# Output tiles of an fp32 batched product, stored head by head instead of with two heads alternating

## The chip, the cores and the metric

The kernel runs on one core of a Trainium2 chip. The metric is the device time of one execution in microseconds (us): before the change the median of three runs is 301.21 us (301.14 to 301.47). Engines are named as in the profile: PE (TensorE matmul), DVE (VectorE), ACT (ScalarE), POOL (GpSimd), SP (SyncE, which here only issues transfers). A "transfer" is one DMA instruction; the core has 16 DMA engines that carry its packets.

## The reference

```python
def setup_inputs():
    batch, n_heads, seq_t, seq_s, channels = 8, 12, 512, 512, 64
    ...
def reference(x, y):
    return np.einsum('bhtc,bhsc->bhts', x, y).astype(np.float32)
```

There are 8 x 12 = 96 heads. For each head, a 512 x 64 matrix x is multiplied by the transpose of a 512 x 64 matrix y, which gives 512 x 512 floats (1 MiB). Inputs are 25.17 MB together, the output is 100.66 MB. The arithmetic runs in bf16 with fp32 sums; inputs and output are fp32 in DRAM.

## The kernel before

**Tiling.** The 96 heads are cut in 6 groups of 16 (`NG`), and each group in two halves of 8 heads, 12 halves in all (`NH`). A load brings one group of x or of y as 128 partitions of 4096 floats: 8 partitions a head (`Q`), 64 rows of 64 channels in each. Each half then makes 4 output tiles (`V`), each for two heads that lie four heads (4 MiB of output) apart; the two are called u = 0 and u = 1. That makes 48 output tiles. An output tile has 128 partitions, and each holds 8 consecutive rows of one head (`K`), 4096 floats or 16 KiB that are contiguous in DRAM. 64 partitions belong to one head of the pair and 64 to the other.

**Staging of x.** ACT casts a loaded x tile to bf16 (`compress`, tile `xk`). `mix` copies it, in four parts of 32 partitions for each half, into `xb`, on POOL for the first two halves and on DVE for the others. `xb` was set to zero once, and each part writes only the places of its own u, so that the matrix has blocks of zeros: one matmul over 128 contraction rows then serves both heads of a pair without mixing them. `transposes` makes `xT` from `xb` on DVE in 32 x 32 blocks of 32-bit words. A word is two bf16 values, and the two stay side by side: before the change they are the places of u = 0 and u = 1, so the columns of `xT`, and with them the rows of an output tile, alternate between the two heads.

**Staging of y.** y tiles are cast to bf16 into `yb` by ACT, DVE and POOL, and DVE transposes them into `yT` in the same manner.

**Products and stores.** PE runs a loop (`all_products`) of 8 matmuls of 128 x 512 for an output tile, four into each of two PSUM buffers (`pm`). ACT copies each buffer into one half of a slot (`result`, 128 x 2048 floats), and SP then stores the whole slot in one transfer of 2 MiB (`store`). There are 5 slots (`SLOTS`); loads and stores share them in turn.

**Order.** The order is written out by hand: loads, casts and mixes of the 12 input tiles, with the first four results woven in, then the rest of the results, four for each half, with `prepare` (transposes of one half, mixes of the next) after every fourth. `emit` derives the semaphore waits from the tiles that an instruction reads and writes. All 60 transfers are issued by SP on one queue, the 12 loads ahead of the 48 stores. A slot is written again by ACT only when the store from it has landed.

**Lines that the change touches.** `ov` (the view of the output that a store writes), `mix` (L123 holds the copy itself), `transposes` (L188 for x, L197 for y), and `products`, which only names what a product reads. The store is issued at L233, the loads at L139; the eviction by ACT is L245, the matmul L223.

Of the kernel before, what the change touches and what calls it, by code (L numbers as in the profile page):

```python
# [9 lines left out]
def kernel(  # L10
# [22 lines left out]
    nc = tc.nc  # L33
    B, H, T, C = x.shape
    _, _, S, _ = y.shape
    P = 128
    G = 16
    Q = P // G
# [3 lines left out]
    V = G // 4  # L42
    K = 8
    E = R // K
    D = 32
# [3 lines left out]
    bf16 = mybir.dt.bfloat16  # L49
# [4 lines left out]
    xv = x.rearrange("b h t c -> (b h t c)").rearrange("(g p n) -> g p n", p=P, n=R * C)  # L54
    yv = y.rearrange("b h t c -> (b h t c)").rearrange("(g p n) -> g p n", p=P, n=R * C)
    ov = out.rearrange("b h t s -> (b h t s)").rearrange(
        "(o u h q n) -> o h q u n", u=2, h=V, q=Q * E, n=K * S
    )

    sb = ctx.enter_context(tc.tile_pool(name="sb", bufs=1))  # L60
# [2 lines left out]
    xks = [sb.tile([P, R, C], bf16, name=f"xk{i}") for i in range(NG - 1)]  # L63
    ybs = [[sb.tile([P, R // 2 * D], u32, name=f"yb{h}{i}") for i in range(NG - 1 + h)] for h in range(2)]
    xbs = [sb.tile([P, K * E * D], u32, name=f"xb{half}") for half in range(2)]
    xTs = [sb.tile([P, K * D * E], u32, name=f"xT{i}") for i in range(2)]
# [5 lines left out]
    def need(name, points, known_by=None):  # L72

        best = {}
        for p, v in points:
            if known[name].get(p, 0) < v:
                best[p] = max(best.get(p, 0), v)
        for p, v in list(best.items()):
            if any(snaps[q, w].get(p, 0) >= v for q, w in best.items() if q != p):
                del best[p]  # L80
        if known_by is not None:
            assert all(p in dict(known_by) and v <= dict(known_by)[p] for p, v in best.items())
        for p, v in best.items():
            if known_by is None:
                engines[name].wait_ge(sems[p], v)  # L85
            known[name][p] = v
            for q, w in snaps[p, v].items():
                known[name][q] = max(known[name].get(q, 0), w)
# [3 lines left out]
    def emit(name, make, reads=(), writes=(), dma=None, lane=None, known_by=None):  # L92

        points = [writer[r] for r in (*reads, *writes) if r in writer]
        points += [v for w in writes for v in readers.get(w, ())]
        if name == "pool" and name in ticks:
            points.append((name, ticks[name]))
        need(name, points, known_by)
        p, step = (lane or name, 1) if dma is None else (f"dma{dma}", 16)
        if p not in sems:  # L100
            sems[p] = tc.alloc_semaphore(p)
        if make is not None:
            make().then_inc(sems[p], step)
        at = (p, ticks.get(p, 0) + step)
        ticks[p] = at[1]
        snaps[at] = {**known[name], p: at[1]}
        if dma is None:
            for q in lanes.get(name, (name,)):
                snaps[at][q] = ticks.get(q, 0)
        for r in reads:  # L110
            readers.setdefault(r, []).append(at)
        for w in writes:
            writer[w], readers[w] = at, []
# [4 lines left out]
    def copy(name, dst, src, reads, writes):  # L118
        emit(
            name,  # L120
            lambda: nc.scalar.activation(dst, src, COPY)  # L121
            if name == "act"
            else engines[name].tensor_copy(dst, src),  # L123
            reads,
            writes,
        )
# [41 lines left out]
    def mix(i, name, part):  # L168

        g, half = divmod(i, 2)  # L170
        ch, u = divmod(part, 2)
        lo = half * 64 + u * D
        xk = g % (NG - 1)
        xv2 = xbs[half].bitcast(bf16).rearrange("p (k e c u) -> p k e c u", k=K, e=E, u=2)
        copy(
            name,
            xv2[part * D:(part + 1) * D, :, :, :, u],
            xks[xk][lo:lo + D, :, ch * D:(ch + 1) * D].rearrange("p (e k) c -> p k e c", k=K),
            [("xk", xk)],
            [("xb", half, part)],  # L180
        )

    def transposes(i):
        g, half = divmod(i, 2)
        b = g % (NG - 1 + half)
        emit(
            "dve",
            lambda: nc.vector.transpose(  # L188
                xTs[half].rearrange("p (k r e) -> p k e r", k=K, e=E),
                xbs[half].rearrange("p (k e c) -> p k e c", k=K, e=E),  # L190
            ),
            [("xb", half, part) for part in range(4)],
            [("xT", half)],
        )
        emit(
            "dve",
            lambda: nc.vector.transpose(  # L197
                yTs[half].rearrange("p (r j) -> p j r", r=D),
                ybs[half][b].rearrange("p (j c) -> p j c", c=D),
            ),  # L200
            [("yb", half, b, ch) for ch in range(2)],
            [("yT", half)],
            lane="tr",
        )

    def products(o, k):
        evicted = 2 * o + k // 4 + 1
        emit("pe", None, [("xT", o // V % 2), ("yT", o // V % 2)], [("pm", k // 4)],
             known_by=[("ev", evicted), ("tr", o // V + 1)])

    def all_products():
# [26 lines left out]
    def result(o, s):  # L238

        for k in range(0, K, 4):  # L240
            pm = k // 4
            products(o, k)
            emit(
                "act",
                lambda: nc.scalar.activation(  # L245
                    slots[s][:, k * S:(k + 4) * S], pms[pm].rearrange("p j s -> p (j s)"), COPY
                ),
                [("pm", pm)],
                [("slot", s, pm)],
                lane="ev",  # L250
            )
        store(o, s)

    def prepare(i):

        if i < NH:
            transposes(i)
        if i + 1 < NH:
            for part in range(4):
                mix(i + 1, "dve", part)  # L260

    with tc.tile_critical():  # L262
# [12 lines left out]
        for n in range(2 * NG):  # L275
            if n == 11:
                result(3, slot())
            compress(n)
            mix(n // 4, "pool", n % 4)
            if n == 4:  # L280
                transposes(0)
            if n < 5:
                load(n + SLOTS)
            elif n in (6, 8):
                load(n // 2 + 7)
            elif n < 10:
                front.append(slot())
            if n > 7 and n < 11:
                result(n - 8, front[n - 8])
            if n == 9:  # L290
                transposes(1)
# [38 lines left out]
```

## Time and profile before

| What | Value |
|---|---|
| Median of three runs | 301.21 us (301.14 to 301.47) |
| The profiled execution's own time | 301.22 us |
| Its span, first to last instruction | 299.2 us |
| ACT busy | 211.8 us (71%) |
| DVE busy | 151.9 us (51%) |
| PE busy | 139.6 us (47%) |
| POOL busy | 56.1 us (19%) |
| Moved by DMA | 125.85 MB, mean 421 GB/s |
| One store, issue to landing (median) | 20.8 us |

The profiled execution lies on the median, so its durations can be set against the median directly; 301.22 - 299.2 = 2.0 us lie outside the span. An engine's busy share is a mean over the span. "Issue to landing" of a store contains the time that it stands behind earlier transfers in the queue. A waiting engine is named with what released it.

### The profile page before, as it was taken

The numbers are of one execution on the slowest core, as the hardware profiler recorded it, in microseconds if no ns is written. First come the engines' busy times: TensorE is split into PE (matmuls) and PEld (weight loads), VectorE is DVE, ScalarE is ACT, GpSimd is POOL, SyncE is SP. The second block draws the span as 40 slices with busy tenths as digits, with TensorE's granted clock in tenths as the row PEclk, the third lists the DMA queues.
The fourth block names the chain that finished last, engine by engine and source line by source line (L and its number), as shares of the span: only waits on it lengthen the run. The fifth ranks groups of instructions, "written<-read, shape, count | busy, mean of one in ns | idle before, by whom it ended". The sixth has DMA issues, their size and how long they took to land.

```text
span 299.2 us, 1282 instructions
## 1 busy us (share of the span) xinstructions
PE 139.6 (47%) x384; PEld 36.1 (12%) x384; DVE 151.9 (51%) x73; ACT 211.8 (71%) x109; POOL 56.1 (19%) x23
## 2 busy tenths in 40 slices
PE   0000040547666655566676465666475766473000
PEld 0000010111111111111111111111111111110000
DVE  2167897999839594907609349086291510000000
ACT  1665676999999998686867677777767686868000
POOL 2399999991000000000000000000000000000000
PEclk9999995657789997867756857756957766957555
DMA  7999999999999999999999999999999999999995
GB/s 278 425 436 427 429 427 432 427 429 425 436 436 423 431 436 424 432 438 425 429 440 426 425 438 431 421 427 436 431 425 425 423 431 429 427 425 425 429 427 237
DMA packets 8642, 125.85 MB, mean 421 GB/s; under 512 B 960, under 2 KB 960, under 8 KB 960
## 3 DMA queue, kind: packets, MB, share of 16 engines
q1 hardware_dynamic: 8640, 125.83, 98.9%
q14 instruction: 2, 0.02, 0.0%
HBM read 25.17 MB, written 100.66 MB: 421 GB/s over the span
## 4 chain that ended last, share of the span: by engine, by line
DMA 61%; ACT 23%; issue 4%; PE 2%; DVE 2%; SPq 0%; ACTq 0%
DMA out_dram<-slot 48%; ACT slot L245 20%; DMA slot<-in_y_dram 7%; DMA slot<-in_x_dram 6%; PE pm L223 2%; DVE yb L123 2%; ACT xk L121 1%; ACT yb L121 1%; SPq L139 0%; ACTq L85 0%; SPq L325 0%; SPq L262 0%
## 5 line engine op out<-in xcount | busy, mean ns | idle before, releaser
L245 ACT ACTIVATE slot<-pm 128x2048 f32<-128x2048 f32 x96 | 174.2, 1885 | 43.2 <-DMA out_dram<-slot 42.5
L223 PE MATMUL pm<-yT,xT 128*128 128x512 bf16 x384 | 139.6, 509 | 134.9 <-ACT slot L245 97.8
L188 DVE STREAM_TRANSPOSE xT<-xb 128x2048 uint32<-128x2048 uint32 x12 | 46.7, 3896 | 69.4 <-PE pm L223 67.0
L223 PEld LDWEIGHTS pm<-yT,xT 128*128 128x128 bf16 x384 | 36.1, 115 | 237.5 <-ACT slot L245 161.1
L123 DVE COPY xb<-xk 32x2048 bf16<-32x2048 bf16 x36 | 46.9, 1303 | 1.0
L123 DVE CAST yb<-slot 64x2048 bf16<-64x2048 f32 x12 | 36.2, 3016 | 17.1 <-DMA slot<-in_y_dram 16.8
L123 POOL COPY xb<-xk 32x2048 bf16<-32x2048 bf16 x12 | 36.3, 3022 | 10.5 <-ACT xk L121 9.7
L121 ACT ACTIVATE xk<-slot 128x4096 bf16<-128x4096 f32 x6 | 21.7, 3617 | 16.3 <-DMA slot<-in_x_dram 16.3
L197 DVE STREAM_TRANSPOSE yT<-yb 128x1024 uint32<-128x1024 uint32 x12 | 23.1, 1928 | 0.0
L121 ACT ACTIVATE yb<-slot 64x2048 bf16<-64x2048 f32 x6 | 14.8, 2463 | 5.2 <-DMA slot<-in_y_dram 5.1
L123 POOL CAST yb<-slot 64x2048 bf16<-64x2048 f32 x6 | 17.8, 2973 | 1.3 <-DMA slot<-in_y_dram 0.8
L271 DVE MEMSET xb<- 128x2048 uint32 x1 | 1.8, 1765 | 1.4 <-SPq L262 1.4
L121 ACT ACT_TABLE_LOAD x1 | 1.3, 1283 | 1.0 <-SPq L262 1.0
L271 POOL MEMSET xb<- 128x2048 uint32 x1 | 1.8, 1805 | 0.5 <-SPq L262 0.5
L314 POOL MEMSET const-float32-0.0<- 128x1 f32 x1 | 0.1, 98 | 0.2 <-issue 0.2
L314 POOL MEMSET const-float32-1.0<- 128x1 f32 x1 | 0.1, 98 | 0.0
L314 POOL MEMSET const-bfloat16-1.0<- 128x1 bf16 x1 | 0.1, 98 | 0.0
L314 POOL MEMSET const-uint8-127<- 128x1 uint8 x1 | 0.1, 98 | 0.0
## 6 DMA issues: line engine op xcount, KB each, us to landing
out_dram<-slot SPq DMA_DIRECT2D x48, 2048.0 KB, 20.8
slot<-in_x_dram SPq DMA_DIRECT2D x6, 2048.0 KB, 17.7
slot<-in_y_dram SPq DMA_DIRECT2D x6, 2048.0 KB, 20.8
```

The costliest lines, as they stand in the source:

```text
L121: lambda: nc.scalar.activation(dst, src, COPY)
L123: else engines[name].tensor_copy(dst, src),
L188: lambda: nc.vector.transpose(xTs[half].rearrange("p (k r e) -> p k e r", k=K, e=E), xbs[half].rearrange("p (k e c) -> p k e c", k=K, e=E),),
L197: lambda: nc.vector.transpose(yTs[half].rearrange("p (r j) -> p j r", r=D), ybs[half][b].rearrange("p (j c) -> p j c", c=D),),
L223: last = nc.tensor.matmul(pms[pm][:, b, :], xT[:, 4 * pm + b, h, :], yT[:, h * S:(h + 1) * S], start=True, stop=True,)
L245: lambda: nc.scalar.activation(slots[s][:, k * S:(k + 4) * S], pms[pm].rearrange("p j s -> p (j s)"), COPY),
L271: lambda: engines[name].memset(xbs[half], 0.0),
L314: nc = _bacc.Bacc("TRN2", target_bir_lowering=False, num_devices=1)
```

## The change

An output tile's partitions are put in another order. Before, partition p belonged to head p mod 2 of the pair; after it, partitions 0 to 63 belong to u = 0 and 64 to 127 to u = 1. Three places follow from that:

- The view `ov` that a store writes lists the head first, then the 64 runs of it (2 x 64 runs of 16 KiB), where it listed 64 pairs of runs (64 x 2). In the built program the destination of each of the 48 stores carries the counts 2 x 64 x 4096 where it carried 64 x 2 x 4096; the source is 128 partitions of 4096 floats in both, and the loads are the same in both.
- `mix` writes `xb` so that a 32-bit word holds two rows of the same head (`w`), and the two heads stand in separate blocks of 32 words.
- `transposes` makes `xT` from `xb` with two instructions, one for each head of the pair, of 128 x 1024 words, where one instruction did 128 x 2048. DVE has 12 more instructions in all.

Matmuls, evictions, loads, the y path and the order of everything else stay as they were.

```diff
     ov = out.rearrange("b h t s -> (b h t s)").rearrange(
-        "(o u h q n) -> o h q u n", u=2, h=V, q=Q * E, n=K * S
+        "(o u h q n) -> o h u q n", u=2, h=V, q=Q * E, n=K * S
     )
...
-        xv2 = xbs[half].bitcast(bf16).rearrange("p (k e c u) -> p k e c u", k=K, e=E, u=2)
+        xv2 = xbs[half].bitcast(bf16).rearrange(
+            "p (k e u c w) -> p k e w u c", k=K, e=E // 2, u=2, w=2
+        )
         copy(
             name,
             xv2[part * D:(part + 1) * D, :, :, :, u],
-            xks[xk][lo:lo + D, :, ch * D:(ch + 1) * D].rearrange("p (e k) c -> p k e c", k=K),
+            xks[xk][lo:lo + D, :, ch * D:(ch + 1) * D].rearrange("p (e w k) c -> p k e w c", k=K, w=2),
...
-        emit(
-            "dve",
-            lambda: nc.vector.transpose(
-                xTs[half].rearrange("p (k r e) -> p k e r", k=K, e=E),
-                xbs[half].rearrange("p (k e c) -> p k e c", k=K, e=E),
-            ),
-            [("xb", half, part) for part in range(4)],
-            [("xT", half)],
-        )
+        xT = xTs[half].rearrange("p (k h u q e) -> p k e u h q", k=K, h=V, u=2, e=E // 2)
+        xb = xbs[half].rearrange("p (k e u c) -> p k e u c", k=K, e=E // 2, u=2)
+        for u in range(2):
+            emit(
+                "dve",
+                lambda: nc.vector.transpose(xT[:, :, :, u], xb[:, :, :, u]),
+                [("xb", half, part) for part in range(4)],
+                [("xT", half, u)],
+            )
...
-        emit("pe", None, [("xT", o // V % 2), ("yT", o // V % 2)], [("pm", k // 4)],
+        emit("pe", None, [("xT", o // V % 2, 0), ("xT", o // V % 2, 1), ("yT", o // V % 2)], [("pm", k // 4)],
```

## The prediction, made before the result was known

> **What bounds the kernel now.** I read the page first: the row of DMA in the 40 slices, the DMA queue, and the chain.
>
> ```profile
> span 299.2 us, 1282 instructions
> ...
> DMA  7999999999999999999999999999999999999995
> ...
> DMA packets 8642, 125.85 MB, mean 421 GB/s; under 512 B 960, under 2 KB 960, under 8 KB 960
> ...
> q1 hardware_dynamic: 8640, 125.83, 98.9%
> ...
> DMA 61%; ACT 23%; issue 4%; PE 2%; DVE 2%; SPq 0%; ACTq 0%
> ```
>
> The DMA row is full from the second slice to the last but one, and one queue fills 98.9% of what 16 DMA engines can do in the span. No compute engine is near that; ACT, the busiest, has 71%. The kernel is bound by its transfers, and mostly by stores (100.66 of 125.83 MB).
>
> The packet line also tells how a transfer is shared out. 60 transfers of 2 MiB make 8640 packets: 960 short ones and 7680 long ones, so 16 short and 128 long a transfer. A long packet is one partition's 16 KiB run. The 16 short ones fit one for each DMA engine, which ends its share with the semaphore; the trace has 16 arrivals for each of the 60 semaphore increments. So every transfer is spread over 16 engines, 8 runs each. A long packet takes 0.989 x 299.2 x 16 / 7680 = 0.616 us (an upper figure, the short ones being in it); the packet records have a median of 0.611 and a shortest of 0.608 us.
>
> Next, the stretches of the last microseconds, when the queue runs out (columns: window; length, busy time and instructions of PE, PEld, DVE, ACT, POOL; PE clock, DMA share, GB/s):
>
> ```profile
> 110.00:260.00 150.00, 92.54 (x246) 23.30 (x244) 72.92 (x40) 111.31 (x62) 0.00 (x0) 0.70 1.01 429
> ...
> 297.00:297.60 0.60, 0.00 (x0) 0.00 (x0) 0.00 (x0) 0.00 (x0) 0.00 (x0) 0.50 0.06 27
> ```
>
> In the steady stretch 16 engines move 429 GB/s, 26.8 each. In the last 0.6 us a single engine is at work (a share of 0.06 is one in 16), with the last run of the last store, and it moves 27 GB/s. An engine that is alone goes no faster than one among sixteen: the limit of 0.61 us a run is the engine's own.
>
> Last, the groups that the change touches, the issues, and SP's own order:
>
> ```profile
> L245 ACT ACTIVATE slot<-pm 128x2048 f32<-128x2048 f32 x96 | 174.2, 1885 | 43.2 <-DMA out_dram<-slot 42.5
> L188 DVE STREAM_TRANSPOSE xT<-xb 128x2048 uint32<-128x2048 uint32 x12 | 46.7, 3896 | 69.4 <-PE pm L223 67.0
> L123 DVE COPY xb<-xk 32x2048 bf16<-32x2048 bf16 x36 | 46.9, 1303 | 1.0
> L123 POOL COPY xb<-xk 32x2048 bf16<-32x2048 bf16 x12 | 36.3, 3022 | 10.5 <-ACT xk L121 9.7
> L197 DVE STREAM_TRANSPOSE yT<-yb 128x1024 uint32<-128x1024 uint32 x12 | 23.1, 1928 | 0.0
> ...
> out_dram<-slot SPq DMA_DIRECT2D x48, 2048.0 KB, 20.8
> ```
>
> ```profile
> 51.62 0.33 SPq L139 DMA_DIRECT2D slot<-in_y_dram  x1
> 55.15 222.88 SPq L233 DMA_DIRECT2D out_dram<-slot  x48
> ```
>
> ACT waits 42.5 us in all for stores to free slots, and DVE 67 us for PE, which itself waits for ACT: everything is paced by stores. All loads are issued before the first store. By the semaphore arrivals the last load lands at 62.6 us, the last store at 298.1, so a store costs (298.1 - 62.6) / 48 = 4.91 us: 8 runs of 0.613.
>
> **The change part by part.**
>
> *Transposes of x.* Twelve of 3896 ns go, 24 of half the size come. The y transpose is exactly that size: 1928 ns. Together 24 x 1.928 = 46.3 against 46.7 us: nothing. Words per partition set the price (1.90 ns a word at 2048, 1.88 at 1024) although the two write with different strides, so the new stride should not matter.
>
> *Mixes of x.* 36 on DVE and 12 on POOL, with the same number of elements and the same inner runs of 32 in one more dimension. Lower bound: no change. Upper bound: DVE falls to POOL's 3022 ns, 36 x 1.72 = 62 us more. I take no change (same engine, same inner run). Both are hidden: for one half DVE has 3.9 + 1.9 + 4 x 1.3 = 11.0 us of work (17.9 at the upper bound) while four stores take 19.6. If the stores got faster this cover would thin; nothing here makes them faster.
>
> *Matmuls, evictions, loads.* The same counts and shapes; the permuted columns of xT cost PE nothing, since it reads 128 adjacent columns as before. SP has the same 60 issues; a store's takes 539 ns against 328 for a load, and SP has room for ten times that.
>
> *The stores.* The bytes, the 128 runs of 16 KiB and their number stay; their order in the instruction changes. The record of a store's issue now lists counts of 2 and 64 elements of 16384 bytes, the inner first: 64 outer steps of 2 runs. A load's lists 128. Both outer counts are multiples of 16. After the change the outer count is 2, with 64 runs inside. The trace has no transfer with such a count, so what it does to the sharing has to be bounded. One end: still 16 engines with 8 runs each, 4.91 us a store, nothing changed. Other end: two engines, each with one outer step of 64 runs, 8 x 4.91 = 39.3 us a store. All rows at hand have 16 shares, but in all of them 16 equal shares can be told as so many whole outer steps (8 of 128, 4 of 64); with an outer count of 2 they cannot, unless something cuts the inner count as well. A hardware that shares out whole outer steps gives two. I take two.
>
> [...]
>
> *The sum.* Up to the last load's landing nothing changes: 62.6 us, as the loads keep 16 engines and stand ahead in the queue. Then 48 stores of 39.25 us (8 x 4.906): 1883.8. From the last landing to the end of the span 1.1, outside the span 2.0. 62.6 + 1883.8 + 1.1 + 2.0 = 1949.5 us, taken as **1950 us**, 6.5 times the time before. No bubble between stores: ACT's 3.7 us of evictions refill a slot while four other stores, 157 us, are queued. Bounds of the store: the pitch of single stores in the trace lies between 4.83 and 4.95 us, times 8 gives 38.6 to 39.6, so 1920 to 1967. Unknown is whether 64 runs in a row on one engine have gaps that 8 do not; 1 us a store would give 1998, and about 30 us either way beyond the bounds is my allowance.
>
> **The rivals.**
>
> *Sharing stays at 16 (not slower).* For it: every transfer in this trace has 16 shares, and 128 partitions on the slot side would allow it. Against it: the reason above. Then the order of addresses is all that changes, and 48 x 4.91 stays: 301.2 us. At best every run falls to the shortest packet, 0.608: 48 x (4.91 - 4.87) = 2 us less, 299; at worst every run takes 0.64 us, as the slowest hundredth of the packet records do, 48 x 8 x 0.03 = 12 us more, 313. It decides if a store still lands with 128 runs over 16 engines. A little over half of this case I put within 0.2% of 301.2.
>
> *Another share count.* If the inner 64 is cut in part, say four or eight engines: 62.6 + 48 x 19.6 + 3.1 = 1007 us, or 62.6 + 48 x 9.81 + 3.1 = 537 us. Nothing in the rows speaks for it.
>
> *Two engines at another rate.* Were the 0.61 us a limit shared with other engines, two alone could go up to twice as fast: 62.6 + 942 + 3.1 = 1008 us. The lone engine at 27 GB/s speaks against it. Slower: the slowest long packets at the very start, with all engines cold, take above 1.0 us, and that for every run would give 62.6 + 48 x 64 x 1.0 + 3.1 = 3138 us. The lone run at the end speaks against that too.
>
> **How the numbers follow.** Two engines at about 0.61 us a run: 0.83. Two at another rate: 0.06. Another share count: 0.04. Sixteen as before: 0.07, of which 0.04 within 0.2% (about what a measurement of this kernel can tell from no change), 0.015 faster, 0.015 slower. The first three cases are all slower, so slower is 0.83 + 0.06 + 0.04 + 0.015, about 0.94; same 0.04; faster 0.02. The range is that of the first case, its bounds and allowance together, 1890 to 2000; with it 0.17 for the other cases and a little of the first is left out.
>
> **What the profile after would show.** The DMA row full for the first 62 us, then at one tenth (2 of 16 engines) to the end, at 54 GB/s; 7680 long packets still, but short ones down to 12 x 16 + 48 x 2 = 288; stores 39.2 us apart, issue to landing near 5 x 39.2 - 3.7 = 192 us (a slot's round less its evictions; now 5 x 4.91 - 3.7 = 20.9); ACT's wait for stores above 1500 us; L188's successor at 24 x 1.93. Wrong would be: 960 short packets (sixteen engines still), a store pitch other than 39 us with 288 short packets (the rate), or a compute engine busier than its wait.

## The result, and the profile after

The changed kernel takes 1930.63 us (median of four runs, 1930.53 to 1930.75) where the kernel before takes 301.19 us (301.14 to 301.47). The ratio is 6.409, with a 95% interval of 6.398 to 6.420. The prediction was 1950 us, with a range of 1890 to 2000.

The page of the changed kernel, in the parts shown of the kernel before:

```profile
span 1928.8 us, 1288 instructions
...
DMA  9311111111111111111111111111111111111111
GB/s 405 156 54 54 54 54 54 54 54 54 54 54 55 54 54 54 54 54 54 54 54 54 54 54 54 54 54 54 54 54 54 54 54 54 54 54 54 54 54 52
DMA packets 7970, 125.85 MB, mean 65 GB/s; under 512 B 288, under 2 KB 288, under 8 KB 288
...
q1 hardware_dynamic: 7968, 125.83, 15.3%
...
another core or an unknown queue 76%; ACT 9%; DMA 4%; issue 0%; DVE 0%; PE 0%; SPq 0%; ACTq 0%
...
L247 ACT ACTIVATE slot<-pm 128x2048 f32<-128x2048 f32 x96 | 174.9, 1874 | 1502.3 <-DMA out_dram<-slot 1502.0
...
L193 DVE STREAM_TRANSPOSE xT<-xb 128x1024 uint32<-128x1024 uint32 x24 | 44.7, 1935 | 1226.7 <-PE pm L225 1224.4
...
L123 DVE COPY xb<-xk 32x2048 bf16<-32x2048 bf16 x36 | 46.1, 1281 | 1.0
```

A slice is now 48 us wide. In the first and the start of the second, loads run at the old rate. From the third slice on, the DMA row stands at one tenth and the rate at 54 GB/s, an eighth of the 429 before. The long packets are as many as before (7968 - 288 = 7680, still 16 KiB each); the short ones fell from 960 to 288 = 12 x 16 + 48 x 2. So a load still has 16 shares and a store has two. ACT, whose own work did not grow (174.9 us in this group), waits 1502 us for slots. In the chain, 76% of the span goes to "another core or an unknown queue": the page does not match these stores' landings to their issues, and the wait of ACT, which names `out_dram<-slot`, says what they are. The work that the change touches costs what it did: the mixes 1281 ns instead of 1303, the transposes of x 44.7 us in 24 pieces instead of 46.7 in 12.

### The profile page after: what moved, and what is told of

The parts are those of the page before. It is cut to its first block, busy times and chain, and to the rows that moved or that the text cites. A ratio compares the mean times of both kernels' runs of the same rounds, so it can differ in the third digit from the quotient of the medians.

```text
span 1928.8 us, 1288 instructions
## 1 busy us (share of the span) xinstructions
PE 169.4 (9%) x378; PEld 41.5 (2%) x384; DVE 148.6 (8%) x85; ACT 212.5 (11%) x109; POOL 55.8 (3%) x23
## 3 DMA queue, kind: packets, MB, share of 16 engines
q1 hardware_dynamic: 7968, 125.83, 15.3%
## 4 chain that ended last, share of the span: by engine, by line
another core or an unknown queue 76%; ACT 9%; DMA 4%; issue 0%; DVE 0%; PE 0%; SPq 0%; ACTq 0%
ACT slot L247 9%; DMA out_dram<-slot 2%; DMA slot<-in_y_dram 1%; DMA slot<-in_x_dram 1%; DVE yb L123 0%; ACT yb L121 0%; PE pm L225 0%; SPq L139 0%; ACTq L85 0%; SPq L327 0%; ACT xk L121 0%; SPq L264 0%
## 5 line engine op out<-in xcount | busy, mean ns | idle before, releaser
L247 ACT ACTIVATE slot<-pm 128x2048 f32<-128x2048 f32 x96 | 174.9, 1874 | 1502.3 <-DMA out_dram<-slot 1502.0
L225 PE MATMUL pm<-yT,xT 128*128 128x512 bf16 x378 | 169.4, 613 | 1530.8 <-ACT slot L247 1492.6
L193 DVE STREAM_TRANSPOSE xT<-xb 128x1024 uint32<-128x1024 uint32 x24 | 44.7, 1935 | 1226.7 <-PE pm L225 1224.4
L225 PEld LDWEIGHTS pm<-yT,xT 128*128 128x128 bf16 x384 | 41.5, 130 | 1657.8 <-ACT slot L247 1568.5
L123 DVE COPY xb<-xk 32x2048 bf16<-32x2048 bf16 x36 | 46.1, 1281 | 1.0
```

The source lines that it names most:

```text
L193: lambda: nc.vector.transpose(xT[:, :, :, u], xb[:, :, :, u]),
L225: last = nc.tensor.matmul(pms[pm][:, b, :], xT[:, 4 * pm + b, h, :], yT[:, h * S:(h + 1) * S], start=True, stop=True,)
L247: lambda: nc.scalar.activation(slots[s][:, k * S:(k + 4) * S], pms[pm].rearrange("p j s -> p (j s)"), COPY),
```

## The experiments

All times are of the slowest and only core. The kernel before, run beside these, had medians of 301.07 to 301.35 us. The kernels staging_only, contig and outer32 were run ten times each, two_queues four times, the other variants once; runs of one kernel lay within 0.3% of each other, except for two_queues. In every variant but two_stores and two_queues, output rows land in the places of other rows; the number of bytes and of runs is always the same.

| Run | Counts of a store's destination | Short packets | Time, us |
|---|---|---|---|
| before | 64 x 2 | 960 | 301.19 |
| after | 2 x 64 | 288 | 1930.63 |
| staging_only | 64 x 2 | 960 | 301.41 |
| view_only | 2 x 64 | 288 | 1930.6 |
| contig | 128 | 960 | 301.36 |
| outer4 | 4 x 32 | 384 | 1006.12 |
| outer8 | 8 x 16 | 576 | 540.22 |
| outer16 | 16 x 8 | 960 | 309.36 |
| outer16_near | 16 x 8 | 960 | 310.59 |
| outer32 | 32 x 4 | 960 | 301.31 |
| outer32_far | 32 x 4 | 960 | 301.26 |
| two_stores | 64, twice | 1728 | 309.05 |
| two_queues | 64, twice | 1728 | 367.63 to 388.17 |

### Each half of the change alone

**The staging without the view** (staging_only), against the changed kernel:

```diff
-        "(o u h q n) -> o h u q n", u=2, h=V, q=Q * E, n=K * S
+        "(o u h q n) -> o h q u n", u=2, h=V, q=Q * E, n=K * S
```

> The changed staging of x (words of two rows of one head, two transposes a half) with the old view for the stores, 64 x 2 runs. The rows of each output tile are therefore written to the places of other rows: the values are permuted, the bytes are the same. Theory (the whole time is in the outermost count of the stores): 16 shares a transfer, 960 short packets, 301.2 us, within 0.2% of the kernel before. Rival (part of the time is in the staging on DVE, off the path only because the stores are so slow): more than 302 us.

301.41 us against 301.35; the ratio is 1.0001 (0.9991 to 1.001). The new mixes and the split transposes cost nothing that can be measured. The rival is out.

**The view without the staging** (view_only), against the kernel before:

```diff
-        "(o u h q n) -> o h q u n", u=2, h=V, q=Q * E, n=K * S
+        "(o u h q n) -> o h u q n", u=2, h=V, q=Q * E, n=K * S
```

> The old staging of x with the new view for the stores, 2 x 64 runs; again rows are written to the places of other rows. Theory: two shares a store, 288 short packets, 38.86 us a store, 1930.6 us as the changed kernel, within 0.2%. Rival: clearly less than 1930 us, the difference being what the staging adds.

1930.6 us, the time of the changed kernel, with the same 288 short packets. The rival is out. One line, the view that the stores write through, holds the whole loss.

### Is it the order of addresses or the outermost count?

**Runs in sequence, with one outer count of 128** (contig), against the kernel before:

```diff
-        "(o u h q n) -> o h q u n", u=2, h=V, q=Q * E, n=K * S
+        "(o h q n) -> o h q n", h=V, q=P, n=K * S
```

> The old staging, and stores whose 128 runs lie one behind the other in DRAM, 2 MiB in one piece, so that the destination has the single outer count 128; rows are written to the places of other rows. Theory (outer count): 16 shares, 301.2 us; the order of addresses is worth nothing, within 0.5%. Rival (runs of one head in sequence are slow to write): clearly slower than 301 us, up to 1930 us.

301.36 us, ratio 0.9999 (0.999 to 1.0009). Stores of 2 MiB in one piece are neither slower nor faster than stores that alternate between places 4 MiB apart.

**Four, eight and sixteen outer steps**, against the kernel before, with c = 4, 8, 16:

```diff
-        "(o u h q n) -> o h q u n", u=2, h=V, q=Q * E, n=K * S
+        "(o u h q n) -> o h u q n", u=c, h=V, q=P // c, n=K * S
```

> The old staging, and stores of 4 x 32 runs, the outer steps 2 MiB apart; rows are written to the places of other rows. Theory (as many engines as the outermost count has steps): 12 x 16 + 48 x 4 = 384 short packets, 32 runs an engine, a store each 19.4 to 19.5 us, 62.4 + 48 x 19.44 + 3.1 = 999 us. Rival (any outer count that is not the old one leaves two engines): 1930 us. Rival (the inner count is cut as well when the outer is short of 16): 301 us.

> The same with 8 x 16 runs, the outer steps 1 MiB apart. Theory: 12 x 16 + 48 x 8 = 576 short packets, 16 runs an engine, a store each 9.71 us if a run costs 0.607 us as with two engines, 9.76 if each transfer has a fixed 0.05 us besides, so 531 to 534 us. Rivals: 1930 us or 301 us, as in the run with 4.

> The same with 16 x 8 runs, the outer steps 512 KiB apart. Theory: all 16 engines, 960 short packets, 8 runs each, a store each 4.91 us, 301.3 us within 0.2%. Rival (something in a two-level destination with few outer steps is slow by itself): above 305 us.

The short packets are 384, 576 and 960, as many shares as outer steps. The steady stretches show it in the rate (columns: window; length, busy time and instructions of PE, PEld, DVE, ACT, POOL; PE clock, DMA share, GB/s). With 2 outer steps (the changed kernel):

```profile
100.00:1900.00 1800.00, 155.37 (x346) 37.87 (x352) 89.25 (x59) 166.49 (x91) 0.00 (x0) 0.52 0.13 54
```

With 4:

```profile
100.00:1000.00 900.00, 151.15 (x339) 36.51 (x337) 90.92 (x50) 156.75 (x86) 0.00 (x0) 0.54 0.25 108
```

With 8:

```profile
100.00:530.00 430.00, 145.07 (x320) 34.58 (x320) 88.88 (x50) 148.09 (x82) 0.00 (x0) 0.57 0.50 216
```

And the kernel before, with 64:

```profile
100.00:290.00 190.00, 107.69 (x292) 27.51 (x292) 81.25 (x44) 134.95 (x75) 0.00 (x0) 0.70 1.01 429
```

54, 108 and 216 GB/s are 27.0 for each of 2, 4 and 8 engines, and the DMA shares of 0.13, 0.25 and 0.50 are 2, 4 and 8 sixteenths. In these runs the number of engines at work is the number of outer steps, up to 16: with 16 steps and with 64 the share is near 1 and the short packets are 960. All the counts tried are powers of two, so what a count such as 12 or 24 gives is not shown. Both rivals (1930 us whatever the count; 301 us by cutting the inner count) are out.

The totals, though, are 6 to 9 us above what the count gives: 1006 for 999, 540 for 531 to 534, and 309.4 for 301.3 although all 16 engines work. For the run with 16 the expected time was thus missed, and the rival's (above 305 us) came. That is a second effect, and the windows of the run with 16 place it:

```profile
62.00:70.00 8.00, 4.35 (x11) 1.02 (x9) 7.73 (x3) 6.53 (x4) 6.39 (x3) 0.79 1.05 305
70.00:78.00 8.00, 2.97 (x10) 0.78 (x10) 7.82 (x4) 7.95 (x5) 0.00 (x0) 0.69 0.97 301
78.00:86.00 8.00, 6.87 (x19) 1.84 (x20) 3.10 (x3) 7.76 (x5) 0.00 (x0) 0.67 0.99 383
86.00:100.00 14.00, 8.52 (x30) 2.46 (x29) 10.71 (x6) 11.94 (x7) 0.00 (x0) 0.89 1.00 422
100.00:200.00 100.00, 62.54 (x163) 15.55 (x160) 54.01 (x30) 74.50 (x41) 0.00 (x0) 0.69 1.01 427
```

The engines are as busy as ever (share near 1) but move 300 GB/s where the kernel before moves 428 to 434:

```profile
62.00:70.00 8.00, 4.48 (x11) 1.02 (x9) 7.84 (x3) 7.79 (x4) 6.48 (x3) 0.50 1.00 428
70.00:78.00 8.00, 3.67 (x13) 0.95 (x12) 7.43 (x4) 7.95 (x5) 0.00 (x0) 0.93 1.02 434
```

In the packet records 120 runs between 62 and 86 us take above 1.0 us (34 and 51 with 4 and 8 outer steps); in the kernel before no run after the loads does. In this stretch the runs together take 90 us more than 0.611 us each, which over 16 engines is 5.6 us on average, and some engines lose more than others. By the semaphore arrivals, of which the last of the 16 counts, the fourth store lands 8.2 us later than in the kernel before, at 90 us, and the lag stays between 8.1 and 8.5 us from there to the last store: the whole loss arises in the first four stores.

### Where the 8 us come from

**Two transfers for a store** (two_stores), against the changed kernel:

```diff
-        emit(
-            "sp",
-            lambda: nc.sync.dma_start(ov[i, h], slots[s]),
-            reads=both(s),
-            dma=s,
-        )
+        for u in range(2):
+            emit(
+                "sp",
+                lambda: nc.sync.dma_start(ov[i, h][u], slots[s][u * 64:(u + 1) * 64]),
+                reads=both(s),
+                dma=s,
+            )
```

> The changed kernel, whole and with its rows in place, but each store is issued as two transfers, one for each head: 64 partitions and 64 runs, so that the outermost count is 64 on both sides. Theory: 16 shares for each of the 96 transfers, 12 x 16 + 96 x 16 = 1728 short packets, far below 1930 us. If a run costs an engine 0.61 us wherever it comes from, a pair costs 8 runs and one more short packet, 4.9 to 5.0 us, and the time is 301 to 306 us. If instead 64 partitions of a slot can be read at half the rate only, a pair costs 9.8 us and the time is near 536 us. [...] Rival (the cost lies in the order of addresses, one head's runs written in sequence): near 1930 us, since that order is kept.

309.05 us, between the two cases. With the new tile kept whole and its rows in place, the outer count of 64 on both sides brings back 1621.6 of the 1629.4 us that the change costs. But neither the flat 0.61 us a run nor half the rate throughout is what happens. The same windows:

```profile
62.00:70.00 8.00, 4.48 (x11) 1.02 (x9) 7.61 (x3) 6.75 (x4) 6.25 (x3) 0.50 1.03 307
70.00:78.00 8.00, 2.64 (x10) 0.75 (x10) 7.57 (x5) 7.95 (x5) 0.00 (x0) 0.93 0.98 293
78.00:86.00 8.00, 6.07 (x20) 1.65 (x18) 3.29 (x3) 7.79 (x5) 0.00 (x0) 0.83 0.99 389
86.00:100.00 14.00, 7.38 (x29) 2.17 (x28) 10.64 (x7) 11.90 (x8) 0.00 (x0) 1.00 1.01 430
100.00:200.00 100.00, 62.05 (x160) 15.61 (x160) 53.52 (x35) 74.37 (x42) 0.00 (x0) 0.69 1.01 427
```

The rate is about 300 GB/s for 16 us, 389 in the next 8 us, and then full. In those 24 us, packet records show runs of up to 1.5 us, more than twice the usual time, beside others of 0.61. The half rate of the expectation (half of 429 is some 215 GB/s) was the author's assumption. The slowest of these windows has 293 GB/s, and from 86 us on, with such transfers still following each other in the one queue, the rate is 427 to 430.

**The two halves on two queues** (two_queues), against the run before:

```diff
             emit(
-                "sp",
-                lambda: nc.sync.dma_start(ov[i, h][u], slots[s][u * 64:(u + 1) * 64]),
+                ("sp", "act")[u],
+                lambda: (nc.sync, nc.scalar)[u].dma_start(ov[i, h][u], slots[s][u * 64:(u + 1) * 64]),
                 reads=both(s),
-                dma=s,
+                dma=s + SLOTS * u,
             )
...
-            need(name, [(f"dma{i}", ticks[f"dma{i}"])])
+            need(name, [(f"dma{j}", ticks[f"dma{j}"]) for j in (i, i + SLOTS)])
```

> The changed kernel, whole and with its rows in place; each store is two transfers of 64 partitions as in the run before, but the first is issued by SP and the second by ACT, on a queue of its own. Theory (the 7.7 us that two transfers on one queue lost come from all engines reading the same 64 partitions at a time): with both halves offered side by side the runs of 1.0 us and more between 62 and 86 us go away, DMA moves above 420 GB/s there, and the time is 301 to 303 us; ACT has room for 48 issues of some 0.6 us, 29 us beside its 212. Rival (the loss is a cost of transfers of 1 MiB as such): 309 us again. Rival (ACT becomes the bound, since its evictions wait behind its issues): above 309 us, with ACT busy in all slices.

367.63, 383.32, 383.74 and 388.17 us in four runs: far more scatter than any other kernel here has, but even the fastest is 59 us above two_stores. All three expectations fail; the third had the direction, but ACT is not the bound (55% busy). The profile is of the slowest of the four runs. Its steady stretch has the engines fully busy at a low rate:

```profile
100.00:200.00 100.00, 55.55 (x125) 13.29 (x126) 43.56 (x29) 56.73 (x32) 0.00 (x0) 0.53 1.00 337
```

Runs above 1.0 us, up to 1.65, now go on to the end (1238 of the 5318 from 100 us on), with a mean of 0.80 us a run. In this kernel, offering both halves side by side does not cure the long packet times, they last to the end. So the idea that it is enough to have both halves in flight is wrong; why the long packet times fade on one queue, and why two queues prevent that, is not settled by these runs.

**Thirty-two outer steps, and the distance in DRAM.** Against the kernel before, outer32:

```diff
-        "(o u h q n) -> o h q u n", u=2, h=V, q=Q * E, n=K * S
+        "(o u h q n) -> o h u q n", u=32, h=V, q=P // 32, n=K * S
```

> The old staging, and stores of 32 x 4 runs, the outer steps 256 KiB apart; rows are written to the places of other rows. The three runs with 4, 8 and 16 outer steps each lost 7 to 8 us over the pure count, in runs of 1.0 to 1.5 us between 62 and 86 us, although the run with 16 had all its engines and the kernel before has them too. [...] Rival (a destination of two levels, with outer steps of 256 KiB or more, is slow to start on): 305 to 309 us, with slow runs between 62 and 86 us as with 16.

301.31 us, ratio 0.9997 (0.9987 to 1.0007). The author had expected 301.3 us; the rival, 305 to 309 us, is out. With 32 outer steps the loss is gone, though the shares are 16 of 8 runs in both cases, and no run after 62 us takes above 1.0 us. Two more runs separate the number of outer steps from their distance in DRAM, 256 and 512 KiB, the other way round. outer16_near:

```diff
-        "(o u h q n) -> o h q u n", u=2, h=V, q=Q * E, n=K * S
+        "(o u h q n) -> o h u q n", u=16, h=2, q=8, n=K * S
...
-            lambda: nc.sync.dma_start(ov[i, h], slots[s]),
+            lambda: nc.sync.dma_start(ov[o // 2, o % 2], slots[s]),
```

> The old staging, and stores of 16 x 8 runs whose outer steps lie 256 KiB apart, as in the run with 32 outer steps, where they were 512 KiB apart in the run with 16; rows are written to the places of other rows. Theory (the 7 to 8 us at the start of the stores come from which slot partitions an engine gets, 8 neighbours here): 309 us again, with runs above 1.0 us between 62 and 86 us. Rival (they come from the distance of the engines' places in DRAM, and 512 KiB or more is what it takes): 301 us.

outer32_far is the same edit with u=32, h=8, q=4 and `ov[o // 8, o % 8]`.

> The old staging, and stores of 32 x 4 runs whose outer steps lie 512 KiB apart, as in the run with 16 outer steps; rows are written to the places of other rows. Theory (slot partitions): 301.3 us, no runs above 1.0 us between 62 and 86 us. Rival (distance in DRAM): 309 us.

310.59 and 301.26 us. The same stretch with 16 outer steps 256 KiB apart:

```profile
70.00:78.00 8.00, 4.03 (x10) 0.98 (x10) 7.66 (x4) 7.95 (x5) 0.00 (x0) 0.64 0.97 285
```

and with 32 outer steps 512 KiB apart:

```profile
70.00:78.00 8.00, 3.61 (x13) 0.93 (x12) 7.66 (x4) 7.95 (x5) 0.00 (x0) 0.93 1.02 436
```

Of the two distances neither makes a difference, the number of outer steps does: 309.36 and 310.59 us with 16, 301.31 and 301.26 us with 32. That much is shown. That it acts through the way the 128 runs are cut into shares, and so through the slot's partitions, was the author's guess and is not shown: no record says which engine took which partition.

Two more things are on record. With 2 outer steps no run after 62 us takes above 1.0 us, while with 4, 8 and 16 some do (34, 51 and 120 between 62 and 86 us). And in the run with 16 the engines move apart: the 16 arrivals of one store lie within 1.6 us in the first store, 5.4 us in the fourth, when the rate is nearly full again, and 5.9 us in the last (0.8 to 2.1 us in the kernel before). Neither says where the time of the long runs is lost, at the slot or elsewhere.

## Why the prediction was right, point by point

- **The bound.** Right. The kernel before had no room on the DMA engines, so whatever a store loses shows in full: the ratio of store pitches, 38.86 / 4.906 = 7.9, over loads that stay at 62.5 us, gives the 6.4 of the whole kernel.
- **Transposes and mixes at nothing.** Right: 24 transposes of 1935 ns against the 1928 expected, mixes at 1281 against 1303, and the staging alone at a ratio of 1.0001. The upper bound of 62 us for the mixes was not needed. (POOL mixes the first three halves, 12 of the 48 copies, and not two as the description of the kernel has it; the prediction's counts, 36 and 12, are right.)
- **The stores, two shares instead of sixteen.** Right, and it was the choice on which all else hung. The trace of before could not decide it, since every transfer in it has 16 shares, and the 0.83 was the author's own estimate; the 288 short packets, the DMA share of 0.13 and the series of 2, 4, 8 and 16 outer steps do.
- **The size of a store.** Slightly too long. The prediction took 8 x 4.906 = 39.25 us. By semaphore arrivals a store took (1927.7 - 62.5) / 48 = 38.86. The difference, 0.39 x 48 = 18.7 us, is nearly all of 1949.5 - 1930.6 = 18.9. The mis-sized term is the 0.613 us a run, taken from 16 engines at 26.8 GB/s each. Two, four and eight engines run at 27.0 GB/s each, 0.607 us a run, as the window with the lone engine at 27 GB/s already hinted. Part of what the 0.613 holds besides is seen in the packet records: from 100 us on a run takes 0.614 us on average in the kernel before and 0.611 in the changed one. The rest was not measured apart. Gaps within 64 runs in a row, the unknown that widened the range, were not seen: 64 x 0.607 = 38.85 is all but the whole 38.86.
- **The sum.** 62.5 + 1865.2 + 1.1 to the end of the span, and 2.0 outside it, is 1930.8, the time of the profiled execution (1930.75).
- **SP's issues.** Wrong, without a cost. The prediction priced a store's issue at 539 ns. In the changed kernel it holds SP for a median of 38.2 us (columns: duration in ns, least, median, most; first and last start):

```profile
L235 SPq DMA_DIRECT2D out_dram<-slot x48: 513/38207/74134, 55.1 to 1807.7; - x48
```

  SP has nothing else to do, and a store lands 82 us (median) after its issue ends, more than two stores' time, so the engines do not run dry (54 GB/s from 100 to 1900 us). The landing time that was forecast from the start of the issue, 192 us, was wrong as well: by the semaphore arrivals it is 121 us (median). The forecast had the issue begin as soon as ACT has filled the slot. Five stores of 38.86 us less 3.7 us of evictions are still 191 us, so a filled slot stands about 69 us until SP comes to its store (an estimate from these medians).
- **The rivals.** Sixteen shares in spite of the view: out by 288 packets. Four or eight engines: out by the share of 0.13. Two at another rate: out by the 54 GB/s.

## What to carry to other kernels

When a store's view of DRAM is reordered, look at its outermost count before anything else: in these runs, where only the DRAM side of the stores fell below a count of 64, a store used as many of the 16 DMA engines as that side had outer steps, up to 16 (2, 4, 8 and 16 at DMA shares of 0.13, 0.25, 0.50 and about 1), and a view that reads more naturally (2 x 64 instead of 64 x 2) made the kernel take 6.4 times as long with not one byte or run more. The short packets told the shares at a glance: 288 = 12 x 16 + 48 x 2 in the changed kernel, 960 = 60 x 16 in the one before. If an order is wanted whose outermost count is small, issue one transfer per outer step on one queue rather than one for all; for 2 x 64, the one case tried, that took 309 us instead of 1931.

## What had not been expected of the hardware

- Sixteen engines at work is not the same as sixteen at full rate: with 16 outer steps of 8 runs (or two transfers of 64 partitions) the stores began at about 300 GB/s and took some 24 us to reach 427, 8 us lost, while 32 and 64 outer steps ran at 428 to 436 from the start.
- The same two transfers on two queues never recovered: 337 GB/s in the stretch from 100 to 200 us, 367.6 to 388.2 us in all.
- An issue instruction on SP took 38.2 us (median) where each engine got 64 runs, 18.8 us with 32, and 0.6 us with 16. What holds SP so long is not shown. A kernel whose issuing engine also computes might pay for that; no run here tried it.
